# Operands of the tensor engine on multiples of 512 bytes, in a one-core decoder block in split float32

## The chip, the core and the metric

The kernel runs on one core of one Trainium2 chip. The core has a tensor engine (PE in the profile; PEld is its weight load), a vector engine (DVE), a scalar engine (ACT), GpSimd (POOL), and SyncE (SP), which here issues every DMA. Each engine works through its own instructions in their order and waits for the others at semaphores. On-chip memory (SBUF) has 128 partitions; a tile's address below is its byte address within a partition. A matmul has a stationary operand (128 x 128 here, loaded ahead) and a moving operand, whose columns (128 to 512) stream through; its result goes to a PSUM bank. The metric is the device time of one execution in microseconds (us), the median of several runs.

## What is computed

One layer: a normed input is projected; three mixers (sliding-window attention, forgetting attention "FoX", a gated linear recurrence) work on it, their outputs are gated and merged, and a SwiGLU feed-forward net (FFN) follows. There are 16 meta tokens ahead of 1024 real ones, width 1024, FFN width 2816. Shortened:

```python
u = rms_norm(h, norm_mix[l])
qa, ka, va, qf, kf, vf, fl, xc, yc, gates = jnp.split(u @ w_in[l], split_points, axis=-1)
o_a = swa_sink_attention(qa, ka, va, swa_sinks[l], rel_bias_table)   # 8 heads, 2 key heads, window 128
log_f = log_sigmoid(fl + fox_forget_bias[l])
o_f = forgetting_attention(qf, kf, vf, log_f)                        # causal, bias from cumsum(log_f)
xc = causal_depthwise_conv(xc, conv_w[l], conv_b[l])
o_c = rg_lru(xc, lru_w_r[l], ..., lru_lambda[l]) * gelu(yc)          # h_t = a_t h_{t-1} + ...
merged = sum(sigmoid(gates[g]) * (o[g] @ w_branch[l, g]) for g in range(3))
h = h + merged @ w_out[l]
u = rms_norm(h, norm_ffn[l])
gate_ff, up_ff = jnp.split(u @ w_ffn_in[l], 2, axis=-1)
h = h + (silu(gate_ff) * up_ff) @ w_ffn_out[l]
```

## The kernel before

Every float32 operand of the tensor engine is split into a rounded part (hi) and the exact rest (lo), by `split`: ACT writes hi, DVE writes lo. `mm3` then forms each product as three matmuls, hi x hi, hi x lo and lo x hi. So nearly every matmul row of the profile has line 139, and groups are told apart by the tiles' names.

The stages follow one another, each with tile pools of its own, stacked from the left end of SBUF (constants, weight stream `wp`, the normed input `u`) and from the right end (all that belongs to one stage):

- *Norm and first projections.* The normed tokens, transposed and split, stand in `uh` and `ul`, each in two chunks of 528 and 512 tokens, eight rows of contraction per chunk. Both chunks are tiles of 8 rows of 528 columns.
- *Recurrence, values.* `lru` (four tiles m) runs beside projections and beside the values (`mm_v`). Its gate products take the split convolution `xh`, `xl` and block-diagonal weights `bdh`, `bdl` into banks `sc`; then follow sigmoids, tanh, exp and a root on ACT, a scan and products on DVE, and a split of y (L107, L108).
- *Attention and gate projections.* `main` issues projections (first a gate, then keys `k`, then queries `q`, ...), `side` the attention; `drive` spreads side over main. `k_proj` empties a bank by `split` for both heads into `k` tiles, and copies rows by DMA; `q_proj` does the like with a scale.
- *Branches 0 and 2* read the mixers' outputs back from DRAM scratch `osp` into the tiles `o4` of pools `r3` (`oA`, `oC`), with weights `wb` and gates `sg` streamed; branch 1 (`oF`, pool `bp`) and `w_out` follow.
- *FFN.* For each hidden tile the products `mm_g` and `mm_u` for two halves of tokens; the first half's operand `hl` is in pool `bp` (right), the second's in `mp` (left). The output products `tr_fo` and `sc_fo` have `fh`, `fl` as moving operand.

PSUM has three banks for projections (tag `mm`), two for `sc`, two for `tr`, one for `ob`. A scheduler orders each engine's instructions from the order of the program, and sets a wait wherever a tile lies on bytes that an earlier tile used. Where a pool's tile lies so also sets when it can be written.

The addresses, modulo 512 bytes, in the program before: the stationary operands `wh`, `wl` of all projections and of the FFN at 384; moving operands `uh`, `ul` at every multiple of 64 (a row is 2112 bytes long), `o4` of the branches at 480, `woh`, `wol` at 480, `hl` at 480 in the FFN's first half and 384 in its second, `fh`, `fl` at 480 against a stationary `hl` at 384. In the values the stationary operand is `u` and the moving one `vh`, `vl` at 0 or 256.

Of the kernel before, what the change touches and what calls it, by code (L numbers as in the profile page):

```python
# [17 lines left out]
D = 1024          # model width  # L18
KT = D // P       # contraction tiles of the model width
NM = 16           # meta tokens  # L20
S = 1024          # real tokens
T = NM + S
NB = S // P       # query blocks
W0 = NM + 512     # tokens in the first chunk of u (the second has 512)
# [4 lines left out]
SCALE = 0.125     # head_dim ** -0.5  # L29

# feature-major column tiles of w_in, in the order in which the host lays them out
QA, KA, QF, KF, XC, YC, GT = 0, 4, 5, 9, 13, 17, 21
# columns of the packed per-channel parameters
P_CW, P_CB, P_BR, P_BI, P_LM, P_NF = 0, 16, 20, 24, 28, 32
# ns of projections between two pieces of the recurrence, of sliding-window and of forgetting attention
LRU_GAP = 3500.0
GAPS = (850.0, 480.0)
CREDIT = 8        # gaps that a wait for a projection may prepay
LAG = 2           # groups of transposed probabilities ahead of their products with the values
# keys of a FoX query block, in pieces that fit a PSUM bank  # L40
FOX_PIECES = [[144], [272], [400], [264, 264], [328, 328], [392, 392], [456, 456], [348, 346, 346]]
# [7 lines left out]
def hybrid_block(ctx, tc, h_in, w_in, w_v0, w_v1, w_bd, par, rows, gains, relt, onehot,  # L49
# [6 lines left out]

    cp = ctx.enter_context(tc.tile_pool(name="const", bufs=1, side="left"))
    wp = ctx.enter_context(tc.tile_pool(name="wstream", bufs=2, side="left"))
    zp = ctx.enter_context(tc.tile_pool(name="z", bufs=2, side="left"))
    ctxu = ctx.enter_context(ExitStack())  # L60
# [4 lines left out]

    uid = [0]

    def nm(s):
        uid[0] += 1
        return f"{s}_{uid[0]}"  # L70
# [33 lines left out]
    def split(hi, lo, src, scale=None, pin=False):  # L104
        """hi = src rounded to float32r, lo = src - hi exactly."""
# [26 lines left out]
    def mm3(ps, terms):  # L132
        """Accumulates a.T @ b over terms (ah, al, bh, bl), three products each."""
# [13 lines left out]
    def log_sigmoid(dst, z, pl, shape):  # L147
        """dst = log_sigmoid(z) = min(z, 0) - log1p(exp(-|z|)), log1p by the atanh series."""
# [15 lines left out]
    def rstd_from(q, n):  # L164
        """1 / sqrt(mean(x^2) + eps) of each row from its partial sums of squares, the last of them late."""
# [11 lines left out]
    def rstd_of(x, n, junk):  # L177
        """rstd_from of the rows of the two halves in x."""
        q = cp.tile([P, 2], F32, tag="sq2", bufs=4, name=nm("sq"))
        for i in range(2):  # L180
            act.activation(junk[i], x[i], AF.Square, accum_out=q[:n, i:i + 1])
        return rstd_from(q, n)
# [4 lines left out]
    def to_feature_major(xg, n, uh, ul, off):  # L187
        """Transposes a token tile into the split columns off:off+n of uh, ul."""
# [8 lines left out]

    uh = [up.tile([P, KT, W0], F32R, tag="u", name=f"uh{c}") for c in range(2)]
    ul = [up.tile([P, KT, W0], F32R, tag="u", name=f"ul{c}") for c in range(2)]
    FULL = ((0, 0, 264, 0), (0, 264, 264, 264), (1, 0, 512, 528))   # chunk, offset, width, token  # L200
# [14 lines left out]
    # Projections (main) and recurrence or attention (side) share the tensor engine: both are  # L215
    # generators, and the side's pieces are spread over the main's matmuls.
    done = set()

    def drive(main, side, gap):
        """Runs both to the end, with gap ns of main work between the pieces of side work."""  # L220
# [21 lines left out]
    # ================= norm, first projections =================  # L242
# [15 lines left out]
    ra = ctx1.enter_context(tc.tile_pool(name="ra", bufs=1, side="right", reuse_waits="tile"))  # L258
    with tc.tile_pool(name="r0", bufs=1, side="right", reuse_waits="tile") as r0:
# [34 lines left out]
        # relative bias by distance, then skewed to [query, key] through DRAM  # L294
# [31 lines left out]
        dma(bts, mr)  # L326
# [670 lines left out]
```

## Time and profile before

| | |
|---|---|
| time, median of three runs | 1763.77 us (1762.84 to 1764.04) |
| span of the profiled execution | 1761.7 us |
| time around the span (difference) | 2.1 us |
| recurrence and values end, attention begins | about 205 to 235 us |
| last gate projection, branches begin | 783 us |
| FFN | 1015 to 1722 us |

The profile is of one execution. Its page gives busy times by engine, the chain of work that ended last, and groups of instructions; windows, groups by form, the timeline (each instruction in order of its start, with the idle time ahead of it and what ended it) and the DMA view are further answers of the same trace. A group's row reads: line, engine, operation, tile written <- tiles read, partitions x columns, count; then busy time and mean duration. Matmuls overlap in their pipeline, so the duration of one (some 0.39 us) is longer than the time from its start to the next one's.

### The profile page before, as it was taken

Reading aid. Unit: us, or ns where it says so; the run is one execution under the profiler, and the core shown is the slowest. Engines: PE = TensorE matmul, PEld = TensorE weight load, DVE = VectorE, ACT = ScalarE, POOL = GpSimd, SP = SyncE. Lnnn points to the kernel's source line nnn. Section 1 sums busy time; section 2 is a strip of 40 time slices with the busy share of each in tenths; the row PEclk is TensorE's granted clock in tenths of the full one; section 3 lists DMA queues with packets and bytes.
Section 4 is the critical chain, followed back from the end, with each engine's and each line's share of the span. In section 5 each row is a group of like instructions: output and inputs, shape, how many; then the busy total and the mean of one; then the engine's idle time right before and its main releaser. Section 6 shows DMA issues by size and latency. Waiting matters only on the chain.

```text
span 1761.7 us, 22267 instructions
## 1 busy us (share of the span) xinstructions
PE 1734.6 (98%) x8537; PEld 1443.8 (82%) x8537; DVE 868.4 (49%) x1746; ACT 647.2 (37%) x1228; POOL 192.4 (11%) x188
## 2 busy tenths in 40 slices
PE   7999999999999999999999999999999999999997
PEld 6898878888888888888878888888888888888885
DVE  6466565555666666414484434424424434434435
ACT  6455565554555555423363331111211211211214
POOL 2111020010222221102340000000000000000004
PEclk9999999999999999999999999999999999999999
DMA  7223242222332323386362241211211211211202
GB/s 256 67 96 107 105 143 96 103 89 84 113 103 81 115 77 107 101 316 237 128 211 86 82 168 36 72 36 36 72 36 36 72 36 36 72 36 36 72 12 96
DMA packets 70122, 170.35 MB, mean 97 GB/s; under 512 B 7416, under 2 KB 19016, under 8 KB 69760
## 3 DMA queue, kind: packets, MB, share of 16 engines
q1 hardware_dynamic: 70016, 168.93, 28.2%
q8 instruction: 67, 1.10, 0.3%
q14 instruction: 39, 0.32, 0.1%
HBM read 123.08 MB, written 40.49 MB: 93 GB/s over the span
## 4 chain that ended last, share of the span: by engine, by line
PE 88%; DVE 5%; issue 4%; ACT 2%; POOL 1%; DMA 0%; SPq 0%; DVEq 0%; POOLq 0%; ACTq 0%
PE mm_w L139 25%; PE mm_g L139 14%; PE mm_u L139 14%; PE tr_fo L139 7%; PE sc_fo L139 7%; PE mm_br L139 6%; PE mm_wo L139 5%; PE ob L524 3%; PE tr L535 3%; PE mm_v L139 2%; PE sc L609 1%; PE sc L610 1%; DVE o L869 1%; PE tr L193 1%; PE tr L849 0%
## 5 line engine op out<-in xcount | busy, mean ns | idle before, releaser
L139 PE MATMUL mm_w<-uh,wh 128*128 128x512 f32 (+1 forms) x744 | 293.3, 394 | 0.0
L139 PE MATMUL mm_w<-uh,wl 128*128 128x512 f32 (+1 forms) x744 | 281.9, 379 | 0.0
L139 PE MATMUL mm_w<-ul,wh 128*128 128x512 f32 (+1 forms) x744 | 281.0, 378 | 0.0
L139 PE MATMUL mm_g<-hl,wh 128*128 128x512 f32 x704 | 219.6, 393 | 0.0
L139 PE MATMUL mm_u<-hl,wh 128*128 128x512 f32 x704 | 218.4, 391 | 0.0
L108 DVE TENSOR_TENSOR wl<-wr,wh 128x1024 fp32r<-128x1024 f32 x85 | 104.2, 1225 | 164.3 <-ACT wh L107 163.1
L107 ACT ACTIVATE wh<-wr 128x1024 fp32r<-128x1024 f32 x85 | 90.0, 1059 | 215.9 <-PE mm_g L139 82.7
L139 PEld LDWEIGHTS mm_w<-uh,wl 128*128 128x128 f32 x744 | 139.9, 188 | 26.3
L139 PEld LDWEIGHTS mm_g<-hl,wh 128*128 128x128 f32 x704 | 132.2, 188 | 30.8
L139 PEld LDWEIGHTS mm_u<-hl,wh 128*128 128x128 f32 x704 | 132.2, 188 | 30.2
L139 PEld LDWEIGHTS mm_w<-uh,wh 128*128 128x128 f32 x744 | 140.2, 188 | 14.2
L139 PEld LDWEIGHTS mm_w<-ul,wh 128*128 128x128 f32 x744 | 140.5, 189 | 12.9
L139 PE MATMUL mm_u<-hl,wl 128*128 128x512 f32 x352 | 138.6, 394 | 0.0
L139 PE MATMUL mm_g<-hl,wl 128*128 128x512 f32 x352 | 138.6, 394 | 0.0
L885 ACT ACTIVATE sg<-mm_g 128x512 f32<-128x512 f32 x44 | 26.0, 591 | 298.7 <-PE mm_g L139 298.6
L139 PE MATMUL tr_fo<-fh,hl 128*128 128x512 f32 (+1 forms) x356 | 125.9, 394 | 0.0
L139 PE MATMUL sc_fo<-fh,hl 128*128 128x512 f32 (+1 forms) x352 | 124.7, 395 | 0.5 <-DVE re L172 0.5
L139 PE MATMUL mm_br<-o,wh 128*128 128x512 f32 x384 | 120.9, 396 | 0.0
L108 DVE TENSOR_TENSOR pl<-tr,ph 128x384 fp32r<-128x384 f32 (+2 forms) x160 | 87.7, 555 | 45.0 <-ACT ph L107 43.7
L919 POOL TENSOR_TENSOR o<-acc,gfc 128x512 f32<-128x512 f32 x15 | 19.4, 1315 | 812.2 <-DVE acc L912 807.1
L887 DVE TENSOR_TENSOR sg<-mm_u,sg 128x512 f32<-128x512 f32 x44 | 30.4, 692 | 151.4 <-PE mm_u L139 151.4
L107 ACT ACTIVATE ph<-tr 128x384 fp32r<-128x384 f32 (+2 forms) x160 | 77.0, 485 | 50.1 <-PE tr L535 48.6
(207 smaller groups left out, 3165.9 us busy)
## 6 DMA issues: line engine op xcount, KB each, us to landing
wr<-w_in_dram SPq DMA_DIRECT2D x45, 512.0 KB, 3.4
wr<-w_fi_dram SPq DMA_DIRECT2D x44, 512.0 KB, 3.6
gz<-z SPq DMA_DIRECT2D x48, 256.0 KB, 2.2
o<-osp SPq DMA_DIRECT2D x24, 512.0 KB, 5.8
sg<-gz SPq DMA_DIRECT2D x48, 256.0 KB, 3.1
for<-w_fo_dram SPq DMA_DIRECT2D x22, 512.0 KB, 3.5
wb<-w_br_dram SPq DMA_DIRECT2D x24, 256.0 KB, 3.5
k<-k SPq DMA_DIRECT2D x20, 260.0 KB, 3.7
```

The costliest lines, as they stand in the source:

```text
L107: act.activation(hi, src, AF.Copy)
L108: i = dve.tensor_tensor(lo, src, f32(hi), ALU.subtract)
L139: pe.matmul(ps, a, b, start=i == 0, stop=i == n - 1)
L193: pe.transpose(pt[:, i * P:i * P + n], xg[:n, k * P:(k + 1) * P], ident[:n, :n])
L524: pe.matmul(ob[:, q0:q0 + b - a], vt[:, c], x[:, a:b], start=count == 0, stop=count == n_mm - 1, skip_group_check=True)
L535: pe.transpose(tb[:, col:col + P], src, ident)
L609: pe.matmul(sc[:, :n], qs, kh[:, k0:k0 + n], start=True, stop=False)
L610: pe.matmul(sc[:, :n], qs, kl[:, k0:k0 + n], start=False, stop=True)
L869: dve.tensor_scalar(o[1], o[1], r, None, ALU.mult)
L885: act.activation(sg, pg, AF.Sigmoid)
L887: dve.tensor_tensor(sg, pv, sg, ALU.mult)
L919: pool.tensor_tensor(g, acc[tt][:, n], gfc[:, n], ALU.mult)
```

## The change

The change puts nearly all operands of the tensor engine on multiples of 512 bytes (some rows on multiples of 256):

- `pad` allocates bytes that nothing uses, in six pools, so that what lies beyond begins on a multiple of 512.
- `u`: chunk 0 gets a tile of its own tag with 112 + 8 x 576 words and 16 behind them, so that a row is 2304 bytes long, and the real tokens, behind the 16 meta tokens, begin on a multiple of 256; chunk 1 has rows of 512 columns.
- Projections of the whole sequence use pieces of 272, 256 and 512 tokens, in place of 264, 264 and 512; the recurrence's gate products likewise; FoX scores use pieces that begin on multiples of 128 real tokens.
- The values' weights get rows of 384 columns of which 320 or 328 are used; the keys get 112 words ahead of them.
- Scratch tiles shared: the spilled halves of the head sums use the buffers of the probabilities (`ph`, `pl`, three each) in place of `oh`, `ol`; the sliding-window bias uses the FoX bias's tile (`nb`); the head sum is formed in its place in `ot`, without a scratch tile; the constant of the cumulative sum has one column, read again and again.

In the program after it, the moving operands `uh`, `ul` of the 512-column projections are at 0 or 256, all others named above at 0, and the stationary ones at 0. At 192, 256 or 448 stay the pieces of 272 columns, the first piece of each FoX block, the recurrence's operands and, in the values, part of the stationary `u`. The number of matmuls is the same, 8536. The left end of SBUF, constants to `u`, is 3200 bytes longer: it ends at 118272, before at 115072.

```diff
-W0 = NM + 512     # tokens in the first chunk of u (the second has 512)
+W0 = NM + 512
+WS = 576
+VS = 384
+LINE = 512
+LEAD = LINE // 4 - NM
...
-FOX_PIECES = [[144], [272], [400], [264, 264], [328, 328], [392, 392], [456, 456], [348, 346, 346]]
+FOX_PIECES = [[144], [272], [400], [272, 256], [272, 384], [400, 384], [400, 512], [272, 384, 384]]
...
+    def pad(pool, n):
+
+        pool.tile([P, n // 4], F32, name=f"pad{uid[0]}")
+        uid[0] += 1
...
+    edge = ctx.enter_context(tc.tile_pool(name="edge", bufs=1, side="right"))
+    pad(edge, LINE - 32)
+    pad(cp, 128)
...
-    uh = [up.tile([P, KT, W0], F32R, tag="u", name=f"uh{c}") for c in range(2)]
-    ul = [up.tile([P, KT, W0], F32R, tag="u", name=f"ul{c}") for c in range(2)]
-    FULL = ((0, 0, 264, 0), (0, 264, 264, 264), (1, 0, 512, 528))   # chunk, offset, width, token
+    def u_tile(c, a):
+        if c:
+            return up.tile([P, KT, 512], F32R, tag="u1", bufs=2, name=f"u{a}1")
+        t = up.tile([P, LEAD + KT * WS + NM], F32R, tag="u0", bufs=2, name=f"u{a}0")
+        return t[:, LEAD:LEAD + KT * WS].rearrange("p (k t) -> p k t", k=KT)
+
+    uh = [u_tile(c, "h") for c in range(2)]
+    ul = [u_tile(c, "l") for c in range(2)]
+    FULL = ((0, 0, 272, 0), (0, 272, 256, 272), (1, 0, 512, 528))
...
     ra = ctx1.enter_context(tc.tile_pool(name="ra", bufs=1, side="right", reuse_waits="tile"))
+    pad(ra, 128)
...
+        pad(r0, 32)
         bb = r0.tile([P, 8, 383], F32, name="bb")
...
-            for t0, n in ((0, 264), (264, 264), (528, 512)):
+            for t0, n in ((0, 272), (272, 256), (528, 512)):
...
         bdh, bdl = load_w(w_bd, D, r1, "bd")
-        # c * log_sigmoid(lambda), and its negative half
+        pad(r1, 448)
...
-        one = rv.tile([8, T], F32, name="one")
+        one = rv.tile([8, 1], F32, name="one")
...
-        dve.tensor_tensor_scan(cum, one, cum, 0.0, ALU.mult, ALU.add)
+        dve.tensor_tensor_scan(cum, one.to_broadcast([8, T]), cum, 0.0, ALU.mult, ALU.add)
...
-        vh = rv.tile([P, KT, ncol], F32R, tag="vh", bufs=1, name=nm("vh"))
-        vl = rv.tile([P, KT, ncol], F32R, tag="vl", bufs=1, name=nm("vl"))
+        vh = rv.tile([P, KT, VS], F32R, tag="vh", bufs=1, name=nm("vh"))
+        vl = rv.tile([P, KT, VS], F32R, tag="vl", bufs=1, name=nm("vl"))
+        vh, vl = vh[:, :, :ncol], vl[:, :, :ncol]
...
-            return (rk if tag in "qk" else r2).tile(shape, dt, tag=tag, bufs=bufs, name=nm(tag))
+            if tag == "k":
+                return rk.tile([P, LEAD + T], dt, tag=tag, bufs=bufs, name=nm(tag))[:, LEAD:]
+            return (rk if tag == "q" else r2).tile(shape, dt, tag=tag, bufs=bufs, name=nm(tag))
...
             v = at([P, 9, P], F32R, "v", 2)
+            if h == 0:
+                pad(r2, 320)
...
-            tmp = at([P, 512], F32, "ot", 1)
-            act.activation(tmp[a, :n], ob[b, :n], AF.Copy)
-            dve.tensor_tensor(ot[a, q0:q0 + n], ob[a, :n], tmp[a, :n], ALU.add)
+            o = ot[a, q0:q0 + n]
+            act.activation(o, ob[b, :n], AF.Copy)
+            dve.tensor_tensor(o, ob[a, :n], o, ALU.add)
...
-                oh_, ol_ = at([P, 512], F32R, "oh", 1), at([P, 512], F32R, "ol", 1)
+                oh_, ol_ = at([P, 512], F32R, "ph", 3), at([P, 512], F32R, "pl", 3)
...
-                            bt = at([P, 256], F32, "bt", 2)
+                            bt = at([P, T], F32, "nb", 2)[:, :256]
```

The new addresses also move instructions. The first place is the end of the recurrence, where its last tile (m = 3) runs beside the first key projection `k` and the first queries `q`. DVE before: `x` is the convolution, `xl` its lo part, each `k` row empties a part of a bank `mm_w` of the key projection, and rows of L377 to L382 end the recurrence (`y` is its output).

```order
L350 SCALAR_TENSOR_TENSOR x_1798<-xr_845,part,x_1798 128x1040
L108 TENSOR_TENSOR k_1933<-mm_w_249_1942,k_1932 64x264
L350 SCALAR_TENSOR_TENSOR x_1798<-xr_845,part,x_1798 128x1040
L108 TENSOR_TENSOR k_1935<-mm_w_249_1942,k_1934 64x264
L350 SCALAR_TENSOR_TENSOR x_1798<-xr_845,part,x_1798 128x1040
L108 TENSOR_TENSOR k_1933<-mm_w_250_1971,k_1932 64x264
L108 TENSOR_TENSOR xl_1804<-x_1798,xh_1803 128x1040
L108 TENSOR_TENSOR k_1935<-mm_w_250_1971,k_1934 64x264
L108 TENSOR_TENSOR k_1933<-mm_w_251_2000,k_1932 64x512
L108 TENSOR_TENSOR wl_2102<-wr_2099,wh_2101 128x1024
L377 SCALAR_TENSOR_TENSOR q_1845<-r_1813,q_1845 128x1040
L108 TENSOR_TENSOR k_1935<-mm_w_251_2000,k_1934 64x512
```

DVE with the change, from the same convolution on:

```order
L370 SCALAR_TENSOR_TENSOR x_1806<-xr_853,part,x_1806 128x1040 x3
L120 TENSOR_TENSOR xl_1812<-x_1806,xh_1811 128x1040
L120 TENSOR_TENSOR wl_2110<-wr_2107,wh_2109 128x1024
L397 SCALAR_TENSOR_TENSOR q_1853<-r_1821,q_1853 128x1040
L398 TENSOR_TENSOR g_1822<-q_1853,g_1822 128x1040
L401 SCALAR_TENSOR_TENSOR x_1860<-r_1821,g_1822 128x1040
L402 SCALAR_TENSOR_TENSOR y_854<-x_1860,y_854 128x1024
L120 TENSOR_TENSOR xl_1864<-y_854,xh_1863 128x1024
L120 TENSOR_TENSOR k_1941<-mm_w_254_1950,k_1940 64x272
L120 TENSOR_TENSOR k_1941<-mm_w_255_1979,k_1940 64x256
L120 TENSOR_TENSOR k_1941<-mm_w_256_2008,k_1940 64x512
L120 TENSOR_TENSOR k_1943<-mm_w_254_1950,k_1942 64x272
```

All six `k` rows have moved behind the recurrence's last row, `xl` from `y`. ACT's six `k` rows moved in the same way, behind its `xh` from `y`. On PE the same place reads, with the change (`sc` banks take the recurrence's gate products, `mm_w_262` is the first bank of `q`):

```order
L151 MATMUL sc_1838<-xh_1811,bdh_636 128x272 [waits Activation_49]
L151 MATMUL sc_1838<-xl_1812,bdh_636 128x272
L151 MATMUL sc_1838<-xh_1811,bdl_637 128x272
L151 MATMUL sc_1843<-xh_1811,bdh_636 128x256 [waits Activation_49]
L151 MATMUL sc_1843<-xl_1812,bdh_636 128x256
L151 MATMUL sc_1843<-xh_1811,bdl_637 128x256
L151 MATMUL sc_1848<-xh_1811,bdh_636 128x512 [waits Activation_49]
L151 MATMUL sc_1848<-xl_1812,bdh_636 128x512
L151 MATMUL sc_1848<-xh_1811,bdl_637 128x512
L151 MATMUL mm_w_262_2049<-uh_99,wh_2045 128x512 [waits DVE_49,PE_49]
```

Before, matmuls of `k` and `q` stood between these gate products, and PE's first matmul of `q` waited for no other engine. Now the four gate products after the key projection follow one another, and the first `q` matmul has a wait for DVE: it takes the bank that held the key projection's first piece.

The second place is SP's queue where the branches begin. Before (`o` are the tiles read back from `osp`, `gz<-z` writes the gates of a projection that runs beside, `wb` is the first branch's weights, `sg` its gates):

```order
L55 DMA o_1471_7883<-osp 128x1024 [waits DMAHW7_49]
L55 DMA o_1475_7887<-osp 128x1024 [waits DMAHW0_49]
L55 DMA gz<-z_7736 128x512 [waits DMAHW1_49,Activation_49]
L55 DMA o_1472_7884<-osp 128x1024 [waits DMAHW2_49]
L55 DMA o_1476_7888<-osp 128x1024 [waits DMAHW3_49]
L55 DMA gz<-z_7770 128x512 [waits DMAHW4_49,Activation_49]
L55 DMA o_1473_7885<-osp 128x1024 [waits DMAHW5_49]
L55 DMA o_1477_7889<-osp 128x1024 [waits DMAHW6_49]
L55 DMA o_1474_7886<-osp 128x1024 [waits DMAHW7_49]
L55 DMA gz<-z_7798 128x512 [waits DMAHW0_49,Activation_49]
L55 DMA o_1478_7890<-osp 128x1024 [waits DMAHW1_49]
L55 DMA wb_7915<-w_br_dram 128x512 [waits DMAHW2_49]
```

With the change:

```order
L59 DMA gz<-z_7731 128x512 [waits DMAHW2_49,Activation_49]
L59 DMA gz<-z_7759 128x512 [waits DMAHW3_49,Activation_49]
L59 DMA gz<-z_7793 128x512 [waits DMAHW4_49,Activation_49]
L59 DMA o_1421_7836<-osp 128x1024 [waits DMAHW5_49,PE_49]
L59 DMA gz<-z_7821 128x512 [waits DMAHW6_49,Activation_49]
L59 DMA o_1425_7840<-osp 128x1024 [waits DMAHW7_49]
L59 DMA o_1422_7837<-osp 128x1024 [waits DMAHW0_49]
L59 DMA o_1426_7841<-osp 128x1024 [waits DMAHW1_49]
```

Behind the last of these rows follow twelve more `o` loads of branches 0 and 2, and then `wb`. The gate writes no longer stand between the loads: the loads moved behind all but one of them. The first load, `o_1421`, has a wait for PE. Its tile has the addresses 116224 to 120320, and the second chunk of `ul` ends at 118272 (before, the first tile began at 116704, and `u` ended at 115072). The eight loads of branch 1, which before stood among the branches' own loads, now stand ahead of all this, beside the last projections.

More of the change, by code (lines that the diff above doesn't have):

```diff
@@ L55, in dma @@
         nc.sync.dma_start(f32(dst) if dst.dtype == F32R else dst, f32(src) if src.dtype == F32R else src)
+    def pad(pool, n):
+        pool.tile([P, n // 4], F32, name=f"pad{uid[0]}")
+        uid[0] += 1
+    uid = [0]
     cp = ctx.enter_context(tc.tile_pool(name="const", bufs=1, side="left"))
@@ L64, in hybrid_block @@
     dp = ctx.enter_context(tc.tile_pool(name="dram", bufs=1, space=DRAM))
-    uid = [0]
     def nm(s):
@@ L740, in o_tiles @@
     def o_tiles(pl):
-        return [[pl.tile([P, S], F32R, tag="m4", name=nm("o4")) for k in range(4)] for a in range(2)]
+        return [[pl.tile([P, S], F32R, tag="m4", name=nm("o4")) for k in range(4)]
+                for a in range(2)]
     def load_o(o, g, k):
```

## Prediction, made before the result was known

> **What bounds the kernel now.** I read the header and the chain of the profile first.
>
> ```profile
> span 1761.7 us, 22267 instructions
> PE 1734.6 (98%) x8537; PEld 1443.8 (82%) x8537; DVE 868.4 (49%) x1746; ACT 647.2 (37%) x1228; POOL 192.4 (11%) x188
> PE 88%; DVE 5%; issue 4%; ACT 2%; POOL 1%; DMA 0%; SPq 0%; DVEq 0%; POOLq 0%; ACTq 0%
> ```
>
> TensorE (PE) is busy for 98% of the span and carries the chain that ends last. So the change can only work in two ways: it alters the time that one matmul takes, or it makes PE wait. Next come the windows: busy time and, in brackets, instructions of PE, then of the other engines; behind POOL stands the granted clock.
>
> ```profile
> 160.00:230.00 70.00, 67.64 (x389) 60.36 (x389) 40.21 (x40) 34.63 (x48) 9.17 (x5) 1.00 0.31 106
> 743.00:781.00 38.00, 38.00 (x166) 30.74 (x165) 3.06 (x3) 7.33 (x11) 0.00 (x0) 1.00 0.88 306
> 784.00:866.00 82.00, 82.00 (x353) 65.98 (x352) 31.99 (x44) 26.70 (x45) 19.56 (x14) 1.00 0.60 204
> 1015.00:1722.00 707.00, 707.00 (x3060) 573.48 (x3059) 274.03 (x364) 118.55 (x162) 0.00 (x0) 1.00 0.16 54
> 1722.00:1762.00 40.00, 28.56 (x128) 22.72 (x126) 25.27 (x47) 20.77 (x53) 19.44 (x15) 0.90 0.29 106
> ```
>
> The second to the fourth of these stretches hold nothing but matmuls of 512 columns, and PE has no gap in them. Their time over their count is the start-to-start time of a matmul; two of each count are records that reach in over an edge. Gate projections: 38.00 / 164 = 231.7 ns. Branches: 82.00 / 351 = 233.6 ns. FFN: 707.00 / 3058 = 231.2 ns.
>
> The FFN's mean is made of two rates. Its moving operand lies at 480 bytes past a multiple of 512 for the first half of the tokens, at 384 for the second; the stationary one at 384 for both. Rows of the timeline, first half and then second (start, duration, matmuls):
>
> ```profile
> 1425.06 0.62 PE L139 MATMUL mm_u<-hl,wh 128*128 128x512 f32 x2
> ...
> 1426.46 0.62 PE L139 MATMUL mm_u<-hl,wh 128*128 128x512 f32 x2
> ...
> 1431.97 0.62 PE L139 MATMUL mm_g<-hl,wh 128*128 128x512 f32 x2
> ...
> 1433.33 0.39 PE L139 MATMUL mm_u<-hl,wh 128*128 128x512 f32 x1
> ```
>
> From the first to the second row stand six matmuls: 1.40 us, 233.3 ns each. From the third to the fourth six again: 1.36 us, 226.7 ns each. Same shapes, same engine, clock 1.00 in both: the place of the operands is worth 6.7 ns a matmul. What the trace doesn't hold is a 512-column matmul with both operands at 0, which is what the change makes.
>
> **The change part by part.** *The rate.* The likeliest reading of the two halves is that the moving operand should stand where the stationary one stands (384 with 384 gave the fast rate, 480 with 384 the slow one). After the change both stand at 0 nearly everywhere, so I give every 512-column matmul 226.7 ns. Counts come from the groups by form:
>
> ```profile
> L139 PE MATMUL mm_w<-uh,wh 128*128 128x512 f32 x632 | 260.4, 412 | 0.0
> L139 PE MATMUL mm_br<-o,wh 128*128 128x512 f32 x384 | 120.9, 396 | 0.0
> L139 PE MATMUL mm_wo<-woh,hl 128*128 128x512 f32 x256 | 80.6, 395 | 0.0
> ```
>
> mm_w comes in three products of 632 each: 1896 x (231.7 - 226.7) = 9.5 us. mm_br and mm_wo have half as many again of the third product: 576 x 6.9 = 4.0 us, and 384 x 6.7 = 2.6 us at the slow half's rate. FFN: 3058 x (231.2 - 226.7) = 13.8 us. Sum 29.9 us. For the narrower products (values, 264-column pieces, scores) I add 1 us only, since rows of the values show nothing to win there (below). **Gain: 31 us**; its bounds are 0 (no change at 0/0) and 79 (rival A).
>
> *The keys behind the recurrence.* ACT and DVE now empty the banks of the first key projection (k) only behind the last step of the recurrence (the order above). Three banks serve the projections; k fills all of them, and the q projection behind it needs the first again. Until then PE has only the recurrence's own gate products, and the order has no projection left between them. So PE stands still from the last such product until the chain from there through y to k is done. The rows of before, on PE, ACT and DVE:
>
> ```profile
> 220.11 0.39 PE L139 MATMUL sc<-xh,bdl 128*128 128x512 f32 x1
> 220.54 0.69 ACT L368 ACTIVATE g<-sc,part 128x512 f32<-128x512 f32 x1 [0.22 <-PE sc L139]
> 221.24 1.28 ACT L373 ACT_TABLE_LOAD   x1
> 222.54 1.17 ACT L373 ACTIVATE r<-r,lsc 128x1040 f32<-128x1040 f32 x1
> 223.71 1.28 ACT L376 ACT_TABLE_LOAD   x1
> 225.00 1.07 ACT L376 ACTIVATE q<-q 128x1040 f32<-128x1040 f32 x1
> 226.11 1.24 DVE L377 SCALAR_TENSOR_TENSOR q<-r,q 128x1040 f32<-128x1040 f32 x1 [7.22 <-ACT q L376]
> 228.11 1.24 DVE L378 TENSOR_TENSOR g<-q,g 128x1040 f32<-128x1040 f32 x1
> 230.10 2.33 DVE L381 TENSOR_TENSOR_SCAN x<-r,g 128x1040 f32<-128x1040 f32 x1
> 233.18 1.23 DVE L382 SCALAR_TENSOR_TENSOR y<-x,y 128x1024 f32<-128x1024 f32 x1
> 204.11 1.06 ACT L107 ACTIVATE xh<-y 128x1024 fp32r<-128x1024 f32 x1 [0.56 <-DVE y L382]
> 205.99 1.22 DVE L108 TENSOR_TENSOR xl<-y,xh 128x1024 fp32r<-128x1024 f32 x1
> 208.34 0.42 DVE L108 TENSOR_TENSOR k<-mm_w,k 64x264 fp32r<-64x264 f32 x1
> 216.71 0.68 DVE L108 TENSOR_TENSOR k<-mm_w,k 64x512 fp32r<-64x512 f32 x1 [2.06 <-ACT k L107]
> ```
>
> The last product leaves PE's issue slot at 220.11 + 0.23 = 220.3, and ACT is through its two table loads, exp and root at 226.1. Then 1.24 + 1.24 + 2.33 + 1.23 on DVE, nothing between them now, to 232.2; 1.06 (xh) on ACT to 233.3; 1.22 (xl) on DVE to 234.5; the four k rows of DVE up to the second one of the first bank, 3 x 0.42 + 0.68, to 236.4. PE waits 16.1 us. The gate products before it wait for each other's two banks with no projection between, which I put at 1 more: **17 us**. Bounds: 14, if the chain begins 2 us sooner because no k stands in it, and 19. All this was hidden behind q's 11 us and the last third of k; what is late next, the copy of k's rows and the first scores, lies behind the 48 q matmuls and stays hidden.
>
> *The branches' operands behind the last projection.* SP issues every DMA, in order. Before, it issues the sixteen 512 KB loads for branches 0 and 2 beside the projections. After, the first of them has a wait for PE, because its tile overlaps the end of the second chunk of u, which the last projection reads. Behind it in SP's queue stand the other fifteen, the first branch's weights (wb) and its gates. Rows of SP, of DMA in a busy stretch of it, and of the work on wb:
>
> ```profile
> 742.25 0.45 SPq L55 DMA_DIRECT2D o<-osp  x1
> 756.66 1.89 SPq L55 DMA_DIRECT2D o<-osp  x4
> 773.38 0.43 SPq L55 DMA_DIRECT2D o<-osp  x1
> 783.04 0.39 PE L139 MATMUL mm_w<-uh,wl 128*128 128x512 f32 x1
> DMA packets 807, 2.66 MB, mean 332 GB/s; under 512 B 82, under 2 KB 82, under 8 KB 807
> wr<-w_in_dram SPq DMA_DIRECT2D x45, 512.0 KB, 3.4
> L107 ACT ACTIVATE wh<-wb x4: 616/624/632, 779.7 to 795.7; 128x512 fp32r<-128x512 f32 x4
> L108 DVE TENSOR_TENSOR wl<-wb,wh x4: 681/693/990, 780.4 to 796.3; 128x512 fp32r<-128x512 f32 x4
> ```
>
> Loads were issued from 742.25 to 773.8, so they had 40 us of cover; now they have none from 783.3 on. Sixteen issues of 0.47 us (1.89 / 4) are 7.5 us, then wb lands 3.4 us later and is split in 0.62 + 0.69: 12.2 us if bandwidth were no limit. But 16 x 0.524 = 8.39 MB stand ahead of wb. The stretch from 756 to 764 us moved 332 GB/s in the mean, its pauses in issue included: 25.3 us, and with landing and split 28. I take 24, near the upper end, since the loads now come without such pauses, at some 400 GB/s (an estimate): 21 + 2 + 1.3. **Stall 24 us**, bounds 12 and 28. The eight loads of branch 1, which now go early, save nothing: their old places lay beside matmuls.
>
> *The clock after the stalls.* The last 40 us, where PE is busy for 28.56, show a clock of 0.90; all stretches without long gaps show 1.00. Two new gaps of 17 and 24 us may each be followed by a few us at a lower clock. Bounds 0 and 4 (0.10 x 40) each; I take 1 each, **2 us**. The Trainium skill, page "TensorE: Matmul & The Clock Gate", section "Part 1: The HAM clock gate", says that PE drops to half its clock after an idle window of about 3.4 us and needs as long to recover. By that rule each gap would cost some 1.7 us (an estimate), 3.4 in all and 1.4 above my term; the row of 0.90 agrees in kind, and no run here shows the size.
>
> *The rest at nothing.* The head sums written in place, spills through the probabilities' buffers, the bias tile in the FoX tile's place, and the constant of one column each keep or shrink their instructions, on ACT, DVE and POOL, which are busy for 37, 49 and 11%: PE covers them; uncovered they would cost about 1 us. The other pieces of projections and scores have the same columns and the same number of matmuls.
>
> **Sum**: -31 + 17 + 24 + 2 = +12 us on the profiled span of 1761.7. Around the span lie 2.1 us (median 1763.8 less 1761.7), so 1775.8, and I round to **1775**.
>
> **Rivals.** *A, faster: 0/0 is better than 384/384.* The step between the two halves is 6.7 ns; another such step gives 220.0 ns. A second gives 213.3, which is also what the columns alone cost: values of 320 columns start 146.7 ns apart (six of them between these rows), so (226.7 - 146.7) / 192 = 0.417 ns a column, times 512 = 213.3.
>
> ```profile
> 176.46 0.31 PE L139 MATMUL mm_v<-vh,uh 128*128 128x320 f32 x1
> ...
> 177.34 0.31 PE L139 MATMUL mm_v<-vh,uh 128*128 128x320 f32 x1
> ```
>
> Some 5,900 matmuls of 512 columns (1896 + 576 + 384 + 3058) times 6.7 are 40 us more: 1735; two steps are 79 more: 1696. For it speaks that the trace has no such 0/0 matmul at 512. Against it speak these very values: among these six are pairs with both operands at multiples of 256, and they start 0.14 to 0.15 us apart like their neighbours. It turns the sign from 2 ns a matmul below 226.7 on (12 us / 5,900). The Trainium skill, page "TensorE: Matmul & The Clock Gate", section "Back-to-back issue gap", gives N / 2.4 + 2.5 ns for a warm array, 215.7 for 512 columns. By it the sum would be 5,900 x 11 = 65 us lower (an estimate), 1710; the trace has 226.7 at best and so doesn't bear it out, but at other addresses than those to come.
>
> *B, the stalls are small.* wb and the loads share the bandwidth so that the first branch can begin early (12 us), the chain of the recurrence begins 2 us sooner (14), and the clock holds: -31 + 14 + 12 = -5, 1759; with the shorter stall at the branches alone -31 + 17 + 12 + 2 = 0, 1764. Against it: wb stands last in the queue, and all its rows of before landed in the order of issue.
>
> *C, the padding does nothing for the rate*, because phases other than the one I named set it; the gate projections, whose moving rows walk through all phases in steps of 64, have 231.7, near the slow half. Then +43: 1807.
>
> **How the numbers follow.** Forecast 0.45 (1766 to 1786: stalls of 31 to 51 us together, clock 2). A 0.33: 0.18 for one step and 0.15 for two. B 0.10, C 0.12. What this kernel's measurement can tell from no change is about 0.2%, 3.5 us: faster is below 1760.2, slower above 1767.3. Faster: A and a third of B, 0.36. Same: the rest of B and the lower edge of the forecast, 0.10. Slower: 0.54. The range runs from 1700 to 1796: it leaves out C (0.12) and about half of A's two steps (0.08).
>
> **What would show it.** In the FFN's window, 707 us should become 693; 231 again would be C, 673 or less would be A. In the timeline of PE one gap of about 16 us should stand at 216 to 236 us, released by DVE's k, and one of about 24 near 780, released by wl or wb. If the second gap is about 12, bandwidth was not the limit. If neither gap is there, the order on SP and DVE doesn't tell what I read from it, and the time is 1733.

## The result, and the profile after

The changed kernel takes 1787.28 us (median of four runs, 1786.19 to 1788.82), the kernel before 1763.30 us beside it (1762.68 to 1764.04): ratio 1.0137, 95% interval 1.0122 to 1.0151. It is slower by 24.0 us, where 11 had been forecast. The header and the chain of the profile after:

```profile
span 1784.4 us, 22239 instructions
PE 1713.3 (96%) x8537; PEld 1444.6 (81%) x8537; DVE 864.5 (48%) x1746; ACT 646.4 (36%) x1228; POOL 192.8 (11%) x188
PE 85%; DVE 6%; issue 4%; ACT 3%; DMA 2%; POOL 1%; SPq 0%; POOLq 0%; ACTq 0%; DVEq 0%
```

PE is busy for 21.3 us less than before, in a span that is 22.7 us longer: its matmuls got faster, and it waits for some 44 us more. The view of PE's waits (what was waited for; us in total, times, longest) tells where. The longest wait before, and the two longest now:

```profile
PE tr L193 <- DVE xg L283: 9.2, 1, 9.2
```

```profile
PE mm_br L151 <- ACT wh L119: 26.0, 1, 26.0
PE mm_w L151 <- DVE k L120: 16.3, 1, 16.3
```

These two hold nearly all of it, and they stand at the two places that the order showed: the first branch and the first queries. The first one's timeline, PE's end of the recurrence and begin of the queries:

```profile
216.32 0.40 PE L151 MATMUL sc<-xh,bdl 128*128 128x512 f32 x1
233.00 0.77 PE L151 MATMUL mm_w<-uh,wh 128*128 128x512 f32 x1 [16.29 <-DVE k L120]
233.56 0.63 PE L151 MATMUL mm_w<-ul,wh 128*128 128x512 f32 x1
233.99 0.63 PE L151 MATMUL mm_w<-uh,wl 128*128 128x512 f32 x1
...
236.55 0.40 PE L151 MATMUL mm_w<-uh,wl 128*128 128x512 f32 x1
236.78 0.39 PE L151 MATMUL mm_w<-uh,wh 128*128 128x512 f32 x1
```

Behind the gap the first matmul takes 0.56 us to the next one's start and seven more 0.43; those from 236.55 on take 0.23: PE comes back at half its rate. Behind the second gap eleven matmuls are slow. The second gap on SP and PE, with the DMA view of 798 to 822 us:

```profile
796.13 0.32 SPq L59 DMA_DIRECT2D o<-osp  x1
797.41 13.76 SPq L59 DMA_DIRECT2D o<-osp  x15
812.09 0.33 SPq L59 DMA_DIRECT2D wb<-w_br_dram  x1
795.94 0.39 PE L151 MATMUL mm_w<-uh,wl 128*128 128x512 f32 x1
821.60 0.63 ACT L119 ACTIVATE wh<-wb 128x512 fp32r<-128x512 f32 x1 [24.59 <-DMA wb<-w_br_dram]
822.29 1.22 PE L151 MATMUL mm_br<-o,wh 128*128 128x512 f32 x2 [25.96 <-ACT wh L119]
DMA packets 2940, 9.45 MB, mean 394 GB/s; under 512 B 325, under 2 KB 325, under 8 KB 2939
```

The first load is issued with the last projection matmul, the other fifteen behind it, and wb at 812.09; it lands at 821.6, behind all sixteen. And the rate, in windows of gate projections, of branches 0 and 2 and of the FFN:

```profile
757.00:793.00 36.00, 36.00 (x161) 29.81 (x160) 2.45 (x2) 6.08 (x9) 0.00 (x0) 1.00 0.63 218
826.00:908.00 82.00, 82.00 (x361) 67.85 (x360) 30.29 (x45) 26.77 (x44) 20.75 (x14) 0.99 0.42 134
1060.00:1750.00 690.00, 690.00 (x3046) 571.35 (x3045) 269.81 (x359) 114.70 (x155) 0.00 (x0) 1.00 0.16 53
```

With two records at the edges taken off, the projections now start 226.4 ns apart (before 231.7) and the FFN's matmuls 226.7 (before 231.2). The branches' window still holds the last slow matmuls and has 228.4 (before 233.6).

### The profile page after: what moved, and what is told of

Read it like the earlier page. It is cut to its first block, busy times and chain, and to the rows that moved or that the text cites. A ratio compares the mean times of both kernels' runs of the same rounds, so it can differ in the third digit from the quotient of the medians.

```text
span 1784.4 us, 22239 instructions
## 1 busy us (share of the span) xinstructions
PE 1713.3 (96%) x8537; PEld 1444.6 (81%) x8537; DVE 864.5 (48%) x1746; ACT 646.4 (36%) x1228; POOL 192.8 (11%) x188
## 4 chain that ended last, share of the span: by engine, by line
PE 85%; DVE 6%; issue 4%; ACT 3%; DMA 2%; POOL 1%; SPq 0%; POOLq 0%; ACTq 0%; DVEq 0%
PE mm_w L151 24%; PE mm_g L151 13%; PE mm_u L151 13%; PE sc_fo L151 6%; PE tr_fo L151 6%; PE mm_br L151 5%; PE mm_wo L151 5%; PE ob L550 3%; PE tr L561 3%; PE mm_v L151 2%; PE sc L635 1%; PE sc L636 1%; DMA o<-osp 1%; DVE o L896 1%; DMA wb<-w_br_dram 1%
## 5 line engine op out<-in xcount | busy, mean ns | idle before, releaser
L151 PE MATMUL mm_w<-uh,wh 128*128 128x512 f32 (+2 forms) x744 | 293.6, 395 | 16.3 <-DVE k L120 16.3
L151 PE MATMUL mm_w<-uh,wl 128*128 128x512 f32 (+2 forms) x744 | 281.0, 378 | 0.0
L151 PE MATMUL mm_w<-ul,wh 128*128 128x512 f32 (+2 forms) x744 | 280.4, 377 | 0.0
L151 PEld LDWEIGHTS mm_br<-o,wh 128*128 128x128 f32 x384 | 73.0, 191 | 41.5 <-ACT wh L119 26.4
```

What stands on the lines that cost most here:

```text
L151: pe.matmul(ps, a, b, start=i == 0, stop=i == n - 1)
```

## The experiments

Times are medians; each group of runs had runs of the kernel before beside it, on the same chip (1763.6 us for x1 to x4, 1763.5 for x5 to x7, 1764.5 for x9). x8, x10 and x11 were run once each, and only times from one matmul's start to the next are read from them.

**x1, x2, x3: take away the first wait, the second, both.** For the keys, moving the pool that holds keys and queries (`rk`) out of the recurrence's bytes needs 3584 bytes; 512 of them come from the lead of u's first chunk. For the loads, one gate buffer less lets the branches' pool begin behind u.

```diff
-        t = up.tile([P, LEAD + KT * WS + NM], F32R, tag="u0", bufs=2, name=f"u{a}0")
-        return t[:, LEAD:LEAD + KT * WS].rearrange("p (k t) -> p k t", k=KT)
+        t = up.tile([P, 48 + KT * WS + NM], F32R, tag="u0", bufs=2, name=f"u{a}0")
+        return t[:, 48:48 + KT * WS].rearrange("p (k t) -> p k t", k=KT)
...
-                pad(r2, 320)
+                pad(r2, 3904)
```

```diff
-        sgs = [tp.tile([P, 512], F32, tag="sg", bufs=4 if g == 1 else 5, name=nm("sg")) for c in range(2)]
+        sgs = [tp.tile([P, 512], F32, tag="sg", bufs=4, name=nm("sg")) for c in range(2)]
```

> The changed kernel with the pool of keys and queries moved 3584 bytes down, out of the recurrence's pool, and the first chunk of u given 256 bytes less ahead of its rows; all else as changed. Theory 1 (the keys' evacuation stands behind the recurrence only because that pool reaches into the recurrence's): PE's gap of 16.7 us near 212 us goes, with the 8 matmuls at half rate behind it (1.6 us), some 18.5 us in all: 1787.3 - 18.5 = 1769, within 2. Rival (the wait only moves, to the copied rows of the keys or to the queries): less than 8 us are won, 1779 to 1787.

> The changed kernel with four in place of five gate buffers in the branches' pool, which then begins behind the end of u; all else as changed. Theory 1 (the overlap of one tile with u holds back SP's queue): the gap of 26.3 us before the branches goes, with the 11 slow matmuls behind it (2.2 us): 1787.3 - 28 = 1759, within 2. Rival (the loads are late anyway, for bandwidth beside the last projections): a gap of 5 us or more stays, 1764 or more.

> Both edits together. Theory 1: the two gaps are independent, 1787.3 - 46.5 = 1741, within 3, and what is left against the kernel before, some 22 us, is the faster matmuls. Rival (stages trade waits: what one gives back another takes): 1750 or more.

Measured: x1 1769.32 us, x2 1758.54, x3 1740.88; ratios to the kernel before 1.0031 (1.0019 to 1.0043), 0.9971 (0.9960 to 0.9983) and 0.9870 (0.9855 to 0.9885). The longest wait of PE in x1 is the second gap, alone:

```profile
PE mm_br L151 <- ACT wh L119: 26.1, 1, 26.1
```

In x2 it is the first, alone:

```profile
PE mm_w L151 <- DVE k L120: 16.3, 1, 16.3
```

In x3 it is that of the very beginning, which every kernel here has:

```profile
PE tr L205 <- DVE xg L302: 9.3, 1, 9.3
PE mm_br L151 <- DVE wl L120: 1.6, 4, 0.6
```

The first wait costs 1758.5 - 1740.9 = 17.7 us, the second 1769.3 - 1740.9 = 28.4, each with its slow matmuls; neither moved elsewhere. What the change gains by its rate is then 1763.6 - 1740.9 = 22.7 us (that it is the rate is shown part by part below), and -22.7 + 17.7 + 28.4 = 23.4 is within 0.6 us of the 24.0 measured.

**x4: another place than 0.** The kernel before with 96 unused bytes at the right end:

```diff
+    edge = ctx.enter_context(tc.tile_pool(name="edge", bufs=1, side="right"))
+    edge.tile([P, 24], F32, name="edgepad")
```

> The kernel before with one edit: 96 unused bytes at the right end of SBUF, so that the moving operands of FFN, w_out and branches stand at 384 modulo 512, where their stationary operands stand already; u and the attention as before. Theory 1 (what counts is that both operands have the same place modulo 256, not that it is 0): FFN at 226.7 ns a matmul in both its halves and its output products, 14 us less there, 1.7 in w_out, 3 in the branches: 1763.3 - 19 = 1744, within 2. Rival (a multiple of 256 or 512 is needed itself): the first half stays at 233 ns, and the time within 3 us of 1763.

Measured 1744.59 us, ratio 0.9892 (0.9878 to 0.9907). Its FFN in a window:

```profile
1010.00:1700.00 690.00, 690.00 (x3049) 571.35 (x3048) 273.02 (x364) 118.43 (x162) 0.00 (x0) 1.00 0.16 55
```

690.00 / 3047 = 226.5 ns with both operands at 384: no multiple of 512 is needed, nor of 256. Two lines win 19 us, with PE's matmuls in the same order as before.

**x5: u as before, all else as in x3.**

```diff
-    uh = [u_tile(c, "h") for c in range(2)]
-    ul = [u_tile(c, "l") for c in range(2)]
-    FULL = ((0, 0, 272, 0), (0, 272, 256, 272), (1, 0, 512, 528))
+    uh = [up.tile([P, KT, W0], F32R, tag="u", name=f"uh{c}") for c in range(2)]
+    ul = [up.tile([P, KT, W0], F32R, tag="u", name=f"ul{c}") for c in range(2)]
+    FULL = ((0, 0, 264, 0), (0, 264, 264, 264), (1, 0, 512, 528))
```

> The kernel of x3 with u as before the change (rows of 2112 bytes in both chunks, pieces of 264, 264 and 512); all other operands stay on multiples of 512. Theory 1 (between attention's pieces the projections run in threes, and a matmul within the first handful after such a piece doesn't reach the fast rate wherever its operands stand): from the first keys of FoX to the last gate projection the time stays within 2 us of x3's, and the whole is 1743 to 1746, the rest being lost in the first stages and in the unbroken projections at the end. Rival (u's place does pay 5 ns a matmul there too, and other pieces of the change took it back): 5 us or more are lost in that stretch, 1748 or more.

Measured 1744.64 us, ratio 0.9893 (0.9877 to 0.9910). So u's place is worth 1744.64 - 1740.88 = 3.8 us in the whole kernel. A product of the projections with its first and last start (count, least, median and greatest duration ahead of them), in the kernel before:

```profile
L139 PE MATMUL mm_w<-uh,wh x744: 279/394/507, 31.9 to 782.6; 128*128 128x512 f32 x158, 128*128 128x264 f32 x28
```

In x3:

```profile
L151 PE MATMUL mm_w<-uh,wh x744: 277/390/481, 31.2 to 779.0; 128*128 128x512 f32 x158, 128*128 128x272 f32 x14, 128*128 128x256 f32 x14
```

In x5:

```profile
L151 PE MATMUL mm_w<-uh,wh x744: 278/395/484, 31.9 to 782.6; 128*128 128x512 f32 x158, 128*128 128x264 f32 x28
```

From the first to the last of them 750.7 us pass before, 747.8 in x3 and 750.7 in x5: 2.9 us for u, and nothing for keys, values, probabilities and scores. In the midst of FoX even less is seen. The window from 430 to 630 us, before:

```profile
430.00:630.00 200.00, 199.23 (x1184) 172.28 (x1183) 125.72 (x403) 108.91 (x228) 44.48 (x53) 1.00 0.33 101
```

The same of x3:

```profile
430.00:630.00 200.00, 198.75 (x1186) 171.90 (x1185) 128.21 (x413) 110.26 (x232) 45.21 (x54) 1.00 0.34 107
```

The same 200 us hold 1184 matmuls before and 1186 in x3, 0.2% more. The forecast's 5 ns on each of the 464 projections of 512 columns among them would have been 2.3 us, 1.2%. The stretch that was named before the run, from the first keys of FoX to the last gate projection, takes 355.9 us in x3 and 356.8 in x5 (from DVE's first `k` row to PE's last `mm_w` row): 0.9 us apart, within the 2 of theory 1, and the whole time lies in its 1743 to 1746.

**x6: attention's pieces in pairs.** To halve the returns from attention to projections, `drive` skips the projections after every other piece and takes twice the gap after the next:

```diff
         for key in side:
+            if pairs and key is None:
+                n += 1
+                if n % 2:
+                    continue
...
-            while more and credit < gap():
+            w = 2 * gap() if pairs and key is None else gap()
+            while more and credit < w:
                 credit += step()
-            credit = max(credit - gap(), 0)
+            credit = max(credit - w, 0)
```

> The kernel of x3 with attention's pieces set two at a time between the projections and twice the gap between pairs; same work. Theory 1: half as many returns from attention to projections, each of which costs some 40 to 60 ns over the fast rate: about 107 fewer in FoX, 4 to 7 us less, 1734 to 1737, if no engine makes PE wait anew. Rival (the slow matmuls belong to attention's pieces, not to the returns): within 1.5 us of 1741, or later where scores wait for their bank.

Measured 1742.13 us (1740.69 to 1742.80), ratio 0.9878 (0.9863 to 0.9893): no gain. Theory 1 had said 1734 to 1737 and missed; the time is the one that the rival gave, within 1.5 us of 1741. x11 below tests the two apart. From the first FoX queries to the last FoX keys (234.8 us in x3, 235.4 here) the times from each matmul's start to the next sum up to 3.2 us less for projections, but to 3.8 us more for attention's pieces (`ob`, `tr`, `sc`); why these got slower was not traced. And runs of six aren't long enough: the third to fifth matmul of a run still take 229 to 232 ns in the mean.

**x7: the shared scratch tiles alone**, in the kernel before:

```diff
-            tmp = at([P, 512], F32, "ot", 1)
...
+            act.activation(o, ob[b, :n], AF.Copy)
+            dve.tensor_tensor(o, ob[a, :n], o, ALU.add)
...
-                oh_, ol_ = at([P, 512], F32R, "oh", 1), at([P, 512], F32R, "ol", 1)
+                oh_, ol_ = at([P, 512], F32R, "ph", 3), at([P, 512], F32R, "pl", 3)
...
-                            bt = at([P, 256], F32, "bt", 2)
+                            bt = at([P, T], F32, "nb", 2)[:, :256]
```

> The kernel before with only the shared scratch tiles (head sum in place, spills in the probabilities' buffers, bias tile in the FoX tile's place, constant of one column): no padding, no other pieces. Theory 1 (sharing scratch makes attention's pool shorter, so that the pool of keys and queries moves up into the recurrence's, and the keys wait): the same gap of 16 to 17 us and the 8 slow matmuls, 1763.6 + 18.5 = 1782, within 2, and no gap at the branches. Rival (the padding does it): 1763.6 within 2.

Measured 1781.76 us, ratio 1.0104 (1.0089 to 1.0119), with this first row in PE's waits:

```profile
PE mm_w L139 <- DVE k L108: 16.3, 1, 16.3
```

The wait of the keys comes from the shared scratch, without any padding. (x7 also has the constant of one column. So has x9 below, with the bias tile, and there the wait is not seen, so those two alone don't cause it.) Sharing takes 8 KB out of attention's pool, and the pool of keys and queries moves up by as much: it ended at 153888, ends at 162080, and the recurrence's weights begin at 158752. The tile that lies on them is the last of the queries' three. (That the scheduler holds back the keys, whose own tiles lie elsewhere, is seen in the order alone; why it does was not traced further.)

**x8: the stationary operand moved in steps of 64 bytes** through the FFN's hidden tiles:

```diff
-        hi = pl.tile([P, n], F32R, tag=tag + "h", name=nm(tag + "h"), **kw)
+        hi = pl.tile([P, n + e], F32R, tag=tag + "h", name=nm(tag + "h"), **kw)
...
+        hi, lo = hi[:, shift:shift + n], lo[:, shift:shift + n]
...
-                w = [load_w(w_fi[f + NF * i], D) for i in range(2)]
+                w = [load_w(w_fi[f + NF * i], D, shift=16 * (f % 5)) for i in range(2)]
```

> The changed kernel with the FFN's stationary operands (gate and up weights) 0, 64, 128, 192 or 256 bytes further, by hidden tile modulo 5; the moving operand stays at 0. Theory 1 (same place modulo 256): 226.7 ns a matmul at 0 and 256, 231 to 234 at 64, 128 and 192. Rival A (only the moving operand's place counts): 226.7 at all five. Rival B (512, not 256): 256 is slow too.

Measured: windows of 20 us, each within the products of one hidden tile (tiles 4, 5, 6, 7, 8, and last tile 3), with the weights 0, 0, 64, 128, 192 and 192 bytes from the moving operand, modulo 256 (the two buffers of the weights are themselves 256 apart modulo 512):

```profile
1186.00:1206.00 20.00, 20.00 (x90) 16.57 (x89) 4.59 (x6) 2.78 (x4) 0.00 (x0) 1.00 0.02 5
1208.00:1228.00 20.00, 20.00 (x90) 16.57 (x89) 7.44 (x9) 4.97 (x7) 0.00 (x0) 1.00 0.19 59
1252.00:1272.00 20.00, 20.00 (x88) 16.10 (x87) 4.00 (x6) 2.78 (x4) 0.00 (x0) 1.00 0.03 6
1274.00:1294.00 20.00, 20.00 (x87) 16.21 (x87) 7.36 (x9) 4.88 (x7) 0.00 (x0) 1.00 0.17 58
1318.00:1338.00 20.00, 20.00 (x89) 16.43 (x88) 4.49 (x6) 2.77 (x4) 0.00 (x0) 1.00 0.02 7
1143.00:1163.00 20.00, 20.00 (x88) 16.19 (x87) 6.67 (x8) 4.02 (x6) 0.00 (x0) 1.00 0.21 70
```

The first two hold the most. Over all hidden tiles the mean from start to start, of `mm_g` and `mm_u` in PE's timeline, is:

```
weights, modulo 512    0      64     128    192    256    320    384    448
ns per matmul          226.7  233.3  232.3  231.1  226.9  233.3  232.6  231.1
```

Two of eight places are fast, and the row repeats after 256 bytes. With x4 (both at 384) it is the distance that counts: only at 0 modulo 256 is the fast rate seen, as theory 1 says. But the 231.1 at 192 and 448 is the mean of two rates: hidden tiles 3 and 13 have 233.3 ns throughout, tiles 8 and 18 have 228.9, outside the 231 to 234 of theory 1, with the same distance and in the same buffers. So at this distance something else counts too. Tiles 3 and 13 follow directly on a tile at distance 128, tiles 8 and 18 on output products; whether that is the reason was not tested.

**x9: few edits.** The kernel before with the 96 bytes of x4, u as in x1, the constant of one column, the bias tile in the FoX tile's place and four gate buffers; nothing for values, keys, probabilities and scores.

> The kernel before with a few of the change's edits: the 96 bytes at the right end, the padded u with its pieces, the constant of one column, the bias tile in the FoX tile's place, and four gate buffers; values, keys, probabilities and scores as before. Theory 1 (of the change's alignments only those of FFN, w_out, branches and u pay, as x4 and x5 came out alike): 1741, within 1.5 of x3, with no gap at either place. Rival (values, keys and probabilities pay a part too): 1743 or more.

Measured 1739.92 us (1739.00 to 1740.54), ratio 0.9863 (0.9846 to 0.9879). Neither wait is there; the first rows of PE's waits:

```profile
PE tr L195 <- DVE xg L291: 8.9, 1, 8.9
PE mm_v L141 <- DVE vst L110: 1.4, 2, 1.1
```

Theory 1 holds: 1741 within 1.5. x9 is 24.5 us under the kernel before that ran beside it; its ratio is not clear of that of x3 (0.9855 to 0.9885), so the two are the fastest of this study.

**x10, x11: an interruption by itself.** In the FFN, which attention doesn't touch, a transpose follows every three matmuls in odd hidden tiles, and the weights stand 64 bytes off in tiles 2 and 3 modulo 4:

```diff
-                        run(mm3(ps, [(wh[:, k * P:(k + 1) * P], wl[:, k * P:(k + 1) * P], *u2[c][k])
-                                     for k in range(KT)]))
+                        for _ in mm3(ps, [(wh[:, k * P:(k + 1) * P], wl[:, k * P:(k + 1) * P], *u2[c][k])
+                                          for k in range(KT)]):
+                            if f % 2:
+                                tc.keep_in_program_order(pe.transpose(tx[:, :P], cmt, ident))
```

> The changed kernel with extra work in the FFN's gate and up products: for odd hidden tiles a transpose of a constant tile follows every three matmuls, its result unused; for hidden tiles 2 and 3 modulo 4 the stationary operands stand 64 bytes further. Only the start-to-start times within the FFN are read. Theory 1 (after an interruption a matmul does not reach the fast rate, wherever its operands stand): the second of three matmuls between transposes takes 229 ns or more for both places, and the two places differ by less than 2 ns in it; without transposes 226.7 against 233. Rival (attention's own pieces, for their waits or banks, slow the matmuls behind them): with transposes 226.7 for the aligned place and 233 for the other.

> As x10, but each transpose is kept in its place behind three matmuls (in x10 nearly all of them ran in one heap ahead of the FFN's products). Extra work: 352 transposes of a constant tile, results unused. Theory 1 (after an interruption a matmul does not reach the fast rate, wherever its operands stand): the second of three matmuls between transposes takes 229 ns or more at both places, and differs by less than 2 ns between the aligned place and the one 64 bytes further; whole hidden tiles without transposes 226.7 and 233. Rival (attention's own pieces, for their waits or banks, slow the matmuls behind them): with transposes 226.7 at the aligned place and 233 at the other.

x10, without the line that keeps the order, told little: the scheduler ran most transposes in heaps away from the products. Where transposes did stand between its matmuls, the second of three took 231.8 ns aligned (62 of them) and 231.2 apart (51). x11, in PE's timeline, with operands aligned and then 64 bytes apart:

```profile
1078.79 0.71 PE L153 MATMUL mm_g<-hl,wh 128*128 128x512 f32 x2
...
1080.40 0.71 PE L153 MATMUL mm_g<-hl,wh 128*128 128x512 f32 x2
...
1147.97 0.71 PE L153 MATMUL mm_g<-hl,wh 128*128 128x512 f32 x2
...
1149.59 0.71 PE L153 MATMUL mm_g<-hl,wh 128*128 128x512 f32 x2
```

Two rounds of three matmuls and a transpose take 1.61 us aligned, 1.62 apart. The second of the three, from its start to the next, takes 232.5 ns in the mean aligned (186 of them) and 231.8 apart (155); in whole tiles without transposes it is 226.7 and 233.3. Interrupted after three, the place of the operands makes next to no difference. The rival, which had 226.7 against 233 with transposes too, is out; why an interruption has this effect stays open.

## Why the prediction was right or wrong

**The step that failed** is this one: "After the change both stand at 0 nearly everywhere, so I give every 512-column matmul 226.7 ns", and in it the term "1896 x (231.7 - 226.7) = 9.5 us" for the projections. The fast rate was measured in unbroken runs, in the FFN, and given to projections that run in groups of three between attention's pieces. There the mechanism doesn't act: x11 shows 232 ns in groups of three at either place, x5 that all of u's alignment is worth 3.8 us, of which 2.9 lie in the stretch that was to give 9.5. Only projections that run unbroken got it, as those of the window from 757 to 793 us above. In the whole timeline of PE 678 of the 512-column projections (the 1896 of the term and 48 whose weights have other names) stand behind six or more others of their run: from start to start they take 232.3 ns before and 227.1 in x3, 3.5 us in all. The other 1266, times over 260 ns left out, take 231.9 before and 231.3 in x3.

**Gain of the rate**: 31 us forecast, 22.7 found (x3). The FFN gave what was said: its first `mm_g` and last `tr_fo` start 735.1 us apart before and 720.5 in x3, 14.6 against 13.8 forecast. Their rows, before:

```profile
L139 PE MATMUL mm_g<-hl,wh x704: 389/392/478, 1015.7 to 1721.7; 128*128 128x512 f32 x176
L139 PE MATMUL tr_fo<-fh,hl x356: 279/396/399, 1060.9 to 1750.8; 128*128 128x512 f32 x176, 128*128 128x256 f32 x2
```

And in x3:

```profile
L151 PE MATMUL mm_g<-hl,wh x704: 388/389/475, 1007.9 to 1699.4; 128*128 128x512 f32 x176
L151 PE MATMUL tr_fo<-fh,hl x356: 279/389/397, 1052.5 to 1728.4; 128*128 128x512 f32 x176, 128*128 128x256 f32 x2
```

Branches and w_out gave 4.2 of the 6.6 forecast: from the first `mm_br` to the first `mm_g` 232.4 us pass before and 228.2 in x3. With the 3.8 of u that is 22.6 of the 22.7. Here the rate itself came. The window of 784 to 866 us, 233.6 ns before, has 82.00 / 361 = 227.1 ns in x3:

```profile
784.00:866.00 82.00, 82.00 (x363) 67.92 (x362) 30.47 (x45) 26.08 (x43) 21.41 (x15) 1.00 0.58 194
```

But the branches' waits for DVE's wl grew from 0.5 us to the 1.6 shown for x3, and in w_out seven matmuls next to transposes take some 386 ns to the next one's start, where before it was some 307. The terms for them counted the rate alone.

The upper bound of the whole gain, 79 us, was worked out wrongly: rival A's two steps are 79 us on top of the 31, so it should be 110.

**The keys**: right. The wait is where it was put, released by DVE's k, and 16.3 us long against 16.1 worked out for it; with its slow matmuls it costs 17.7 (x2 against x3), where the terms had 17 and 1 for the clock.

**The loads**: right in its mechanism, too small: 24 forecast, 26.0 measured, 28.4 with the slow matmuls (x1 against x3). The loads moved 394 GB/s, as taken. But fifteen issues in a row took 13.76 us, 0.92 each and not 0.47, and wb, whose landing I had put 2 us behind the loads' 21, came 9.5 us after its own issue.

**The clock**: 8 and 11 matmuls at 0.43 in place of 0.23 us are 1.6 and 2.2 us, 3.8 in all; 2 were taken, of bounds 0 and 8. The Trainium skill, "TensorE: Matmul & The Clock Gate", section "Part 1: The HAM clock gate", gave 3.4 in all by its rule of half the clock for a window of about 3.4 us; the trace agrees behind the first gap, where 3.55 us pass from the first slow matmul (233.00) to the first fast one (236.55); behind the second it is longer, 4.8 us (822.29 to 827.11).

**The rivals.** A (0 with 0 is faster still) is out: 226.7 at 0 with 0, as at 384 with 384 in x4. By the rule that the prediction cites from the Trainium skill, "TensorE: Matmul & The Clock Gate", section "Back-to-back issue gap", it would be 215.7; no run here shows that for these operands. B (small waits) is out: the two waits are 42.3 us together. C (no effect of the place) is out for unbroken runs and true for broken ones. The forecast's sign and its range held; its size was 11 us where 24 were found. Some 8 of the difference are missing gain: 5.7 in the projections, nearly all for their broken runs, 2.4 in branches and w_out, 1 in the narrower products, less 0.8 that the FFN gave more. Some 3 are the second wait with its slow matmuls.

## What to carry to other kernels

A rate that was measured in an unbroken run of matmuls need not hold in broken ones, and here it did not; count how many matmuls stand between interruptions before giving it to a stage. Before padding everything, find what the gain hangs on: here the distance of the two operands modulo 256 bytes in a few large stages, which 96 bytes at one end of memory set right for 19 of 23 us. And whatever changes a pool's size moves its neighbours onto others' bytes: read from the order which instructions got a new wait, and what stands behind them in that engine's queue, since one such wait of SP cost more than all alignment won.

## What the runs showed of the hardware that was not expected

- In unbroken runs a 512-column matmul in float32 halves starts 226.7 ns after the one before if stationary and moving operand have the same address modulo 256 (0 with 0, 0 with 256, 384 with 384), and 232 to 233.3 ns at distances of 64 and 128 bytes; at 192 it was 233.3 in two hidden tiles and 228.9 in two others. Multiples of 512 showed no merit of their own.
- After a transpose the second of three such matmuls took 232 ns at either of two distances, 0 and 64 bytes. In FoX of x3 six uninterrupted matmuls go by before the mean is under 228 (four runs are that long); behind the transposes of w_out in x3 it stays under 228 from the eleventh on (eight runs).
- After waits of 16 and 26 us PE ran 8 and 11 matmuls at some 427 ns, and the next ones at 227 to 236.
